# Grouped-query score maps as three fp32r products over 128 rows instead of one plain fp32 product over 64

## The chip, the cores and the metric

The kernel runs on one core of one Trainium2 chip. The metric is the device time of one execution in microseconds (us). TensorE (PE) does the matmuls and the transposes, VectorE (DVE) and ScalarE (ACT) the elementwise work, GpSimd (POOL) small row work and some transfers, and the SyncE (SP) queue the large transfers.

## The reference

Two layers of a hybrid flow-matching backbone on 384 tokens: 256 latent ones (token tiles t=0, 1) and 128 context ones (t=2). Every layer is half a SwiGLU step, a token mixing, and half a SwiGLU step, each between RMS norms that are modulated by a projected condition. What the change touches is the grouped-query part of the mixing:

```python
dq = rms_norm(d_q.reshape(bsz, t, 4, 64), p["gqa_qnorm"][l])   # 4 query heads
dk = rms_norm(d_k.reshape(bsz, t, 2, 64), p["gqa_knorm"][l])   # 2 key heads
# latent tokens: rotary on dq and dk, 128 cached context keys ahead of the own ones
s = jnp.einsum("bqkgd,bskd->bkgqs", qb, k) * 64 ** -0.5
p = jax.nn.softmax(s, axis=-1)
out = jnp.einsum("bkgqs,bskd->bqkgd", p, v)
```

All is float32. Latent queries see 384 keys (128 cached, 256 own), context queries their own 128.

## The kernel before

**Weights.** All weights stream from HBM as 512 KB units on the SP queue (`Stream.load`). ACT casts a unit to fp32r (the high half, L167) and DVE subtracts to get the low half (L168); both write a tile `wu`. A projection is three fp32r matmuls, high by high, high by low and low by high (L556 to L558, L562 to L564, L590 to L592). These fill nearly all of PE's time.

**Order.** A scheduler places each engine's instructions ahead of the run, from the dependences and its own estimates; on an engine they then run in that fixed order, each waiting for semaphores. So the order on an engine is not that of the source.

**The mixing** (`mix`): projections for the convolution branch; then for each token tile the grouped-query projection (into a PSUM tile `ps_j`) and `d_rows`, which squares the rows on ACT (`sqd`), copies the values (`Vg`), sums the squares on DVE (`ss`), gets a reciprocal root on POOL (`rstd`, L470 and L474), scales on DVE (`dn`) and for t<2 applies the rotary on DVE (`dr`, L748 to L757). `d_tail` then transposes the result on PE into a PSUM tile `ps_dT` (L873, L874) and ACT copies it out (L875 queries `qTg` with the scale, L878 keys `kTg`, or `kTgp` for t=2). In `qTg` the two key groups lie on partitions 0 to 63 and 64 to 127. The cached keys come into the first 128 columns of `kTg` by a POOL DMA.

Then twelve units, three token tiles by four heads, software-pipelined over three steps: `probs` makes the score map on PE (`ps_s`, L897), DVE takes the row maximum (L898) and ACT the exponential (`p`, L902); `turned` transposes it (`ps_pT`, L912) and ACT copies (`wt`, L914); `weighted` multiplies with the values (`ps_pv`, L920). Between the units lie the projections of the differential attention (`ps_j`, transposed into `ps_qk`, L1031), and after every unit DVE does four steps of a 31-tap convolution (`cacc`, L825). Twelve units of the differential attention follow, then a norm, and the output projection (`rows_out`).

**Buffers.** `ps_dT`, `ps_pT`, `ps_qk` and some others share two PSUM banks (`mbank`); maps and projections share six (`bank`). Where ACT and DVE both read one PSUM tile, the framework makes the one wait for the other. Sums of squares write their squares to a tile `sink` that nobody reads (L500, L541), and the condition's weights come through two tiles `ast` that DVE multiplies into `acc` (L284, L288).

Of the kernel before, what the change touches and what calls it, by code (L numbers as in the profile page):

```python
# [186 lines left out]
def kernel(ctx: ExitStack, tc: tile.TileContext, a: dict):  # L187
# [7 lines left out]
    ap_ = ctx.enter_context(tc.tile_pool(name="adap", bufs=2))  # L195
# [28 lines left out]
    for t in range(NT):  # L224
# [8 lines left out]
    sink = cp.tile([P, D], BF16, name="sink")  # L233
# [23 lines left out]
    class Ada:  # L257
# [18 lines left out]
        def step(self, pool):  # L276
# [4 lines left out]
            for c in range(2):  # L281
                s1 = sc[:, k, 0, c : c + 1]
# [11 lines left out]
        def finish(self):  # L294
# [13 lines left out]
            else:  # L308
# [12 lines left out]
                grow = tp.tile([P, 512], F32, tag="grow", name=nm("grow"))  # L321
# [76 lines left out]
    def first_mod(q):  # L398
        ps = mbank(nm("ps_first"))
        ws = a0.pop(q)  # L400
        for k in range(KC):
            for s in range(2):
# [3 lines left out]
                    lhsT=sc[:, k, :, :].rearrange("p r i -> p (r i)"),  # L406
# [89 lines left out]
    def pre_norm(t, xn):  # L496
        ss = sm.tile([P, 2], F32, tag="ss", name=nm("ss"))
        for hf in range(2):
            hsl = slice(hf * 512, (hf + 1) * 512)
            nc.scalar.activation(  # L500
                out=sink[:, hsl], in_=x[t][:, hsl], func=AF.Square, scale=D ** -0.5,
                accum_out=ss[:, hf : hf + 1],
            )
# [30 lines left out]
    def post(l, i, t, y):  # L534
# [82 lines left out]
    def ffn(l, i, h, adas, nxt, first=None):  # L617
# [27 lines left out]
        with tc.tile_pool(name=nm("fp"), bufs=1) as fp:  # L645
# [75 lines left out]
    def mix(l, h, nxt):  # L721
        with tc.tile_pool(name=nm("mp"), bufs=1) as mp:
# [13 lines left out]
            nc.gpsimd.dma_start(out=kTg[:, 0:P], in_=a["cache_kT"][l, :, 2])  # L736
# [51 lines left out]
            upad = mp.tile([P, 2, TOK + 3 * CPAD], F32, tag="c3", bufs=4, name=nm("upad"))  # L788
# [22 lines left out]
            cacc = mp.tile([P, 2, TOK + CPAD], F32, tag="c3", bufs=4, name=nm("cacc"))  # L811
# [3 lines left out]
            def conv_some(n):  # L815
                for _ in range(min(n, len(conv_todo))):
# [7 lines left out]
                    else:  # L824
# [3 lines left out]
                        )  # L828

# [104 lines left out]
            def gqa_unit(t, hd, box):  # L934
# [3 lines left out]
                vs = slice(64 * v, 64 * v + 64)  # L938
# [359 lines left out]
```

## Time and profile before

| | |
|---|---|
| median of 3 runs | 1543.93 us (1543.18 to 1545.84) |
| the profiled execution | 1548.72 us, span 1546.9 us |
| granted TensorE clock, mean | 0.993 |
| PE busy | 1492.0 us, 96% |
| DVE busy | 1048.2 us, 68% |
| ACT busy | 635.4 us, 41% |
| POOL busy | 131.4 us, 8% |

The profile is one execution; times in it are us from the start of its span. A group's row gives the line, the engine, the operation, output<-inputs with their shapes, the count, the busy time and the mean of one in ns, then the idle time of the engine just before and what ended it. In a timeline "[1.69 <-DVE dr L757]" behind a row says that the engine sat idle for 1.69 us before it until that instruction released it.

### The profile page before, as it was taken

The page shows a single profiled execution, that of the slowest core. Times are in us where ns is not written, and L with a number is a line of the kernel's source. Part 1 is how long each engine was busy: PE and PEld are TensorE (multiplying, and loading weights), DVE is VectorE, ACT ScalarE, POOL GpSimd, SP SyncE. Part 2 cuts the span into 40 slices and gives each one's busy share as a digit, 9 for nine tenths or more (in the row PEclk, how much of TensorE's full clock was granted, in tenths as well). Part 3 has the DMA queues.
Part 4 walks back from the last instruction along what each step waited for, and adds up shares of the span by engine and source line. Part 5 has one row for each costly group of instructions (what it writes and reads, how often), then busy time and mean ns, then how long its engine had stood idle before and what let it go on. Part 6 is the DMA issues. An engine that isn't in the chain of part 4 may idle for free. (4 is left out here: it accounts for less than half of the span.)

```text
span 1546.9 us, 20700 instructions
## 1 busy us (share of the span) xinstructions
PE 1492.0 (96%) x7924; PEld 1312.3 (85%) x7924; DVE 1048.2 (68%) x1454; ACT 635.4 (41%) x1103; POOL 131.4 (8%) x234
## 2 busy tenths in 40 slices
PE   5999999999999999999999999999999999999997
PEld 3799997777887899998879999887778879999885
DVE  3688889768887846677694666984798785334432
ACT  3442333273575633333263332334545763323331
POOL 1101000021011201000021000001200120000000
PEclk9999999999999999999999999999999999999999
DMA  8678667732224646566655566773322345344431
GB/s 318 231 235 274 228 223 242 242 109 97 69 69 150 204 133 203 201 214 195 197 166 182 183 196 202 234 237 100 124 74 91 108 146 168 123 136 141 134 108 41
DMA packets 73619, 260.13 MB, mean 168 GB/s; under 512 B 9728, under 2 KB 9856, under 8 KB 73520
## 3 DMA queue, kind: packets, MB, share of 16 engines
q1 hardware_dynamic: 68112, 246.32, 48.8%
q0 software_dynamic: 4976, 11.70, 2.8%
q8 instruction: 62, 1.02, 0.3%
q10 hardware_dynamic: 432, 0.79, 0.1%
q14 instruction: 37, 0.30, 0.1%
HBM read 256.36 MB, written 2.41 MB: 167 GB/s over the span
## 5 line engine op out<-in xcount | busy, mean ns | idle before, releaser
L168 DVE TENSOR_TENSOR wu<-st,wu 128x1024 fp32r<-128x1024 f32 x322 | 390.6, 1218 | 258.9 <-ACT wu L167 258.3
L167 ACT CAST wu<-st 128x1024 fp32r<-128x1024 f32 x322 | 337.1, 1052 | 536.2 <-PE ps_f L564 266.4
L562 PE MATMUL ps_f<-h,wu 128*128 128x384 f32 x1248 | 419.0, 336 | 0.0
L564 PE MATMUL ps_f<-h,wu 128*128 128x384 f32 x1248 | 417.1, 334 | 0.0
L563 PE MATMUL ps_f<-h,wu 128*128 128x384 f32 x1248 | 417.1, 334 | 0.0
L288 DVE SCALAR_TENSOR_TENSOR acc<-ast,sc,acc 128x1024 f32<-128x1024 f32 x224 | 279.6, 1281 | 35.0 <-DMA ast<-w_ada 34.6
L562 PEld LDWEIGHTS ps_f<-h,wu 128*128 128x128 f32 x1248 | 234.2, 188 | 7.5 <-issue 7.5
L563 PEld LDWEIGHTS ps_f<-h,wu 128*128 128x128 f32 x1248 | 234.3, 188 | 0.0
L564 PEld LDWEIGHTS ps_f<-h,wu 128*128 128x128 f32 x1248 | 234.2, 188 | 0.0
L590 PE MATMUL ps_o<-wu,hid_s 128*128 128x512 f32 x528 | 207.7, 393 | 0.0
L592 PE MATMUL ps_o<-wu,hid_s 128*128 128x512 f32 x528 | 206.3, 391 | 0.0
L591 PE MATMUL ps_o<-wu,hid_s 128*128 128x512 f32 x528 | 206.2, 391 | 0.0
L590 PEld LDWEIGHTS ps_o<-wu,hid_s 128*128 128x128 f32 x528 | 99.5, 188 | 26.0 <-issue 5.0
L592 PEld LDWEIGHTS ps_o<-wu,hid_s 128*128 128x128 f32 x528 | 99.5, 188 | 21.0
L591 PEld LDWEIGHTS ps_o<-wu,hid_s 128*128 128x128 f32 x528 | 99.6, 189 | 20.3
L702 ACT ACTIVATE sg<-ps_f 128x384 f32<-128x384 f32 x78 | 38.0, 487 | 114.1 <-PE ps_f L564 111.0
L556 PE MATMUL ps_j<-wu,h 128*128 128x512 f32 (+1 forms) x192 | 72.8, 379 | 0.0
L558 PE MATMUL ps_j<-wu,h 128*128 128x512 f32 (+1 forms) x192 | 70.5, 367 | 1.1 <-DVE h L479 1.1
L703 DVE TENSOR_TENSOR hid<-sg,ps_f 128x384 f32<-128x384 f32 x78 | 42.9, 550 | 40.4 <-PE ps_f L564 40.3
L557 PE MATMUL ps_j<-wu,h 128*128 128x512 f32 (+1 forms) x192 | 69.8, 363 | 0.0
L825 DVE SCALAR_TENSOR_TENSOR cacc<-upad,late,cacc 128x399 f32<-128x399 f32 x120 | 69.3, 628 | 0.0
L331 POOL DMA_DIRECT2D gd<-grow x24 | 11.8, 497 | 660.3 <-DVE grow L323 660.3
(234 smaller groups left out, 1698.1 us busy)
## 6 DMA issues: line engine op xcount, KB each, us to landing
st<-ws SPq DMA_DIRECT2D x320, 512.0 KB, 4.3
ast<-w_ada SPq DMA_DIRECT2D x128, 512.0 KB, 4.4
a<-ada SPq DMA_DIRECT2D x16, 512.0 KB, 10.2
G<-gd POOLq DMA_DIRECT2D x12, 512.0 KB, 4.2
brow<-b_ada POOLq DMA_DIRECT2D x24, 64.0 KB, 6.7
prow<-norm_post POOLq DMA_DIRECT2D x24, 64.0 KB, 6.9
x<-x_sample SPq DMA_DIRECT2D x2, 512.0 KB, 5.6
x<-x_prompt SPq DMA_DIRECT2D x1, 512.0 KB, 10.6
```

The lines of the kernel that those rows point to most:

```text
L167: nc.scalar.copy(out=u[:, 0, :], in_=x)
L168: nc.vector.tensor_tensor(out=u[:, 1, :], in0=x, in1=u[:, 0, :].bitcast(F32), op=ALU.subtract)
L288: nc.vector.scalar_tensor_tensor(out=self.acc[c], in0=w, scalar=s1, in1=self.acc[c], op0=ALU.mult, op1=ALU.add)
L556: nc.tensor.matmul(out, lhsT=hk(h, k, 0, tsl), rhs=wh, start=start, stop=False)
L557: nc.tensor.matmul(out, lhsT=hk(h, k, 0, tsl), rhs=wl, start=False, stop=False)
L558: nc.tensor.matmul(out, lhsT=hk(h, k, 1, tsl), rhs=wh, start=False, stop=stop)
L562: nc.tensor.matmul(out, lhsT=wh, rhs=hk(h, k, 0, sl), start=start, stop=False)
L563: nc.tensor.matmul(out, lhsT=wh, rhs=hk(h, k, 1, sl), start=False, stop=False)
L564: nc.tensor.matmul(out, lhsT=wl, rhs=hk(h, k, 0, sl), start=False, stop=stop)
L590: nc.tensor.matmul(out, lhsT=pr[:, 0, s, tsl], rhs=u[:, 0, hsl], start=(q == 0), stop=False)
L591: nc.tensor.matmul(out, lhsT=pr[:, 0, s, tsl], rhs=u[:, 1, hsl], start=False, stop=False)
L592: nc.tensor.matmul(out, lhsT=pr[:, 1, s, tsl], rhs=u[:, 0, hsl], start=False, stop=(q == n - 1))
```

## The change

The score map's queries and keys are kept as fp32r halves (high, low). `qTg` grows to all 128 partitions for each of the four heads: a head's queries lie on its group's 64 partitions and the other 64 hold zeros, which two POOL memsets per layer write at the start of the mixing. `probs` takes lists, and for the grouped-query heads issues three fp32r matmuls, high by high, high by low and low by high, over 128 rows. The differential heads pass lists of one and stay plain fp32.

A helper `halves` makes a pair: ACT writes the high half, DVE subtracts it from the source for the low one. `d_tail` calls it three times per token tile (queries on partitions 0 to 63, queries on 64 to 127, keys) where two ACT copies were; the cached keys come into a tile `kc` and are split once per layer.

To pay for the space, the pool of the `ast` tiles moves from the whole program into `ffn`, `sink` is halved so that both halves of a sum of squares write the same place, `grow` loses its second buffer, and the small tiles `sc` and `upad` are laid out anew.

```diff
-    sink = cp.tile([P, D], BF16, name="sink")
+    sink = cp.tile([P, 512], BF16, name="sink")
...
-        with tc.tile_pool(name=nm("fp"), bufs=1) as fp:
+        with tc.tile_pool(name=nm("fp"), bufs=1) as fp, tc.tile_pool(name=nm("adap"), bufs=2) as ap_:
...
-            kTg = mp.tile([P, TOK], F32, name=nm("kTg"))
-            kTgp = mp.tile([P, P], F32, name=nm("kTgp"))
-            qTg = mp.tile([P, 2, TOK], F32, name=nm("qTg"))
+            kTg = mp.tile([P, 2, TOK], F32R, name=nm("kTg"))
+            kTgp = mp.tile([P, 2, P], F32R, name=nm("kTgp"))
+
+            qTg = mp.tile([P, 2, 4, TOK], F32R, name=nm("qTg"))
+            for v in range(2):
+                z = qTg[64 * (1 - v) : 64 * (1 - v) + 64, :, 2 * v : 2 * v + 2, :]
+                nc.gpsimd.memset(z.bitcast(F32), 0.0)
...
+            def halves(hi, lo, src, scale=1.0):
+                nc.scalar.mul(hi, src, scale)
+                nc.vector.scalar_tensor_tensor(
+                    out=lo, in0=src, scalar=scale, in1=hi.bitcast(F32), op0=ALU.mult, op1=ALU.subtract
+                )
...
+            halves(kTg[:, 0, 0:P], kTg[:, 1, 0:P], kc[:, 0:P])
...
-                nc.scalar.mul(
-                    qTg[:, :, t * P : (t + 1) * P], pt[:, 0:256].rearrange("p (g n) -> p g n", g=2), 64 ** -0.5
-                )
-                nc.scalar.copy(out=kTg[:, (t + 1) * P : (t + 2) * P] if t < 2 else kTgp, in_=pt[:, 256:384])
+                tsl, ksl = slice(t * P, (t + 1) * P), slice((t + 1) * P, (t + 2) * P)
+                for v in range(2):
+                    r, c = slice(64 * v, 64 * v + 64), slice(2 * v, 2 * v + 2)
+                    halves(
+                        qTg[r, 0, c, tsl], qTg[r, 1, c, tsl], pt[r, 0:256].rearrange("p (g n) -> p g n", g=2),
+                        64 ** -0.5,
+                    )
+                k0, k1 = (kTg[:, s, ksl] if t < 2 else kTgp[:, s, :] for s in range(2))
+                halves(k0, k1, pt[:, 256:384])
...
-                nc.tensor.matmul(ps[:, 0:nk], lhsT=lhsT, rhs=rhs, start=True, stop=True)
+                for j, (lt, rt) in enumerate(zip(lhsT, rhs)):
+                    nc.tensor.matmul(ps[:, 0:nk], lhsT=lt, rhs=rt, start=(j == 0), stop=(j == len(rhs) - 1))
...
-                    box[hd] = probs(t, box["st"], hd, qTg[vs, g, tsl], kt[vs, :])
+                    box[hd] = probs(
+                        t, box["st"], hd, [qTg[:, s, hd, tsl] for s in (0, 0, 1)], [kt[:, s, :] for s in (0, 1, 0)]
+                    )
```

The change lets the scheduler order all engines anew. PE, layer 0, where `d_tail` of t=1 and t=2 meets the first maps. Before (ps_dT_3134 is that of t=1, ps_dT_3191 that of t=2, ps_s_3141 and ps_s_3173 the first two maps; L556 to L558 are projections, and the "..." leave out 7 and 10 of them):

```order
L873 MATMUL ps_dT_3134<-early,dr_3048 128x128 x2
L556 MATMUL ps_j_3121<-wu_3111,h_2561 128x512
L557 MATMUL ps_j_3121<-wu_3111,h_2561 128x512
L558 MATMUL ps_j_3121<-wu_3111,h_2561 128x512
L897 MATMUL ps_s_3141<-kTg_2808,qTg_2810 128x384
L556 MATMUL ps_j_3121<-wu_3111,h_2561 128x512
...
L558 MATMUL ps_j_3121<-wu_3116,h_2562 128x512
L897 MATMUL ps_s_3173<-kTg_2808,qTg_2810 128x384
L556 MATMUL ps_j_3178<-wu_2946,h_2559 128x512
...
L558 MATMUL ps_j_3178<-wu_2951,h_2560 128x512
L873 MATMUL ps_dT_3191<-early,dn_3099 128x128 x2
```

The same place in the changed kernel (ps_dT_3146 is t=1, ps_dT_3211 t=2, ps_s_3157 and ps_s_3191 the first two maps; the "..." leaves out 9 projections):

```order
L887 MATMUL ps_dT_3146<-early,dr_3056 128x128 x2
L557 MATMUL ps_j_3133<-wu_3123,h_2563 128x512
...
L558 MATMUL ps_j_3133<-wu_3128,h_2564 128x512
L559 MATMUL ps_j_3133<-wu_3128,h_2564 128x512
L887 MATMUL ps_dT_3211<-early,dn_3111 128x128 x2
L917 MATMUL ps_s_3157<-kTg_2811,qTg_2813 128x384
L917 MATMUL ps_s_3191<-kTg_2811,qTg_2813 128x384
L557 MATMUL ps_j_3198<-wu_2954,h_2561 128x512
L558 MATMUL ps_j_3198<-wu_2954,h_2561 128x512
L917 MATMUL ps_s_3157<-kTg_2811,qTg_2813 128x384 x2
L917 MATMUL ps_s_3191<-kTg_2811,qTg_2813 128x384 x2
```

The transposes of t=2 now stand ahead of the first map, and 12 projections behind those of t=1 instead of 24. DVE at the same place, before (dr_3048 and rt_3049 are the rotary of t=1, ss_3093 and dn_3099 belong to t=2):

```order
L752 TENSOR_TENSOR dr_3048<-dn_3043,late 128x384
L168 TENSOR_TENSOR wu_3116<-st_2944,wu_3116 128x1024
L757 TENSOR_TENSOR dr_3048<-dr_3048,rt_3049 128x384
L840 TENSOR_REDUCE ss_3093<-sqd_3089 128x6
L168 TENSOR_TENSOR wu_3164<-st_2949,wu_3164 128x1024
L846 TENSOR_TENSOR dn_3099<-ps_j_3058,rstd_3097 128x2x2x64
L852 TENSOR_TENSOR dn_3099<-ps_j_3058,rstd_3097 128x128
L857 TENSOR_TENSOR dn_3099<-dn_3099,gqk 128x256
L857 TENSOR_TENSOR dn_3099<-dn_3099,gqk 128x128
L825 SCALAR_TENSOR_TENSOR cacc_2935<-upad_2819,late,cacc_2935 128x399 x2
```

And in the changed kernel (L746 is the low half; ps_dT_3079 is t=0, ps_dT_3146 t=1; "..." leaves out the four dn_3111 rows, which stand as before):

```order
L764 TENSOR_TENSOR dr_3056<-dn_3051,late 128x384
L746 SCALAR_TENSOR_TENSOR qTg_2813<-ps_dT_3079,qTg_2813 64x2x128
L769 TENSOR_TENSOR dr_3056<-dr_3056,rt_3057 128x384
L168 TENSOR_TENSOR wu_3128<-st_2952,wu_3128 128x1024
L746 SCALAR_TENSOR_TENSOR qTg_2813<-ps_dT_3079,qTg_2813 64x2x128
L854 TENSOR_REDUCE ss_3105<-sqd_3101 128x6
L746 SCALAR_TENSOR_TENSOR kTg_2811<-ps_dT_3079,kTg_2811 128x128
L168 TENSOR_TENSOR wu_3182<-st_2957,wu_3182 128x1024
...
L746 SCALAR_TENSOR_TENSOR qTg_2813<-ps_dT_3146,qTg_2813 64x2x128
L837 SCALAR_TENSOR_TENSOR cacc_2941<-upad_2825,late,cacc_2941 128x399
L746 SCALAR_TENSOR_TENSOR qTg_2813<-ps_dT_3146,qTg_2813 64x2x128
L760 TENSOR_TENSOR rt_3177<-ps_j_3133,late 128x32x8 x2
```

The low halves stand between the norm's steps, and the last step of the rotary of t=1 (L769) now stands ahead of a weight unit's low half (L168) instead of behind it. ACT behind the weight cast that follows `Vgp`, with what each row waits for, in the changed kernel (before, the two copies of a token tile stood together and waited for PE only):

```order
L745 ACTIVATE kTg_2811<-ps_dT_3079 128x128 [waits DVE_49]
L745 ACTIVATE qTg_2813<-ps_dT_3146 64x2x128 [waits PE_49]
L745 ACTIVATE qTg_2813<-ps_dT_3146 64x2x128 [waits DVE_49]
L745 ACTIVATE qTg_2813<-ps_dT_3211 64x2x128 [waits PE_49]
L745 ACTIVATE kTg_2811<-ps_dT_3146 128x128 [waits DVE_49]
```

The second high half of a token tile and that of its keys now wait for DVE; the keys of t=1 (the last row), which the first map reads, stand behind the first high half of t=2.

## Rows read from the trace of the kernel before

**Rows 1.** The page: busy time, share of the span and instructions of each engine, and the granted TensorE clock in 40 slices.
```profile
PE 1492.0 (96%) x7924; PEld 1312.3 (85%) x7924; DVE 1048.2 (68%) x1454; ACT 635.4 (41%) x1103; POOL 131.4 (8%) x234
PEclk9999999999999999999999999999999999999999
```

**Rows 2.** PE's waits over the whole run: line, what it waited for, us in total, times, longest.
```profile
PE ps_t L515 <- DVE xn L505: 14.9, 14, 2.7
...
PE ps_dT L873 <- DVE dr L757: 3.4, 2, 1.7
```

**Rows 3.** The score maps, L897, by form (duration in ns min/median/max). The profiler records two passes for each plain fp32 map, so 32 rows are 16 maps of 384 keys and 16 are 8 maps of 128.
```profile
L897 PE MATMUL ps_s<-kTg,qTg x32: 482/535/587, 369.2 to 1151.3; 64*128 64x384 f32 x32
...
L897 PE MATMUL ps_s<-kTgp,qTg x16: 272/322/373, 400.7 to 1166.1; 64*128 64x128 f32 x16
```

**Rows 4.** Timeline of PE at the second map of layer 0: start, duration, instruction.
```profile
371.71 0.39 PE L557 MATMUL ps_j<-wu,h 128*128 128x512 f32 x1
371.94 0.39 PE L558 MATMUL ps_j<-wu,h 128*128 128x512 f32 x1
372.26 0.91 PE L897 MATMUL ps_s<-kTg,qTg 64*128 64x384 f32 x2
373.10 0.50 PE L556 MATMUL ps_j<-wu,h 128*128 128x512 f32 x1
373.43 0.39 PE L557 MATMUL ps_j<-wu,h 128*128 128x512 f32 x1
```

**Rows 5.** Timeline of PE in a SwiGLU stage: fp32r products of 384 columns over 128 rows.
```profile
100.17 0.33 PE L562 MATMUL ps_f<-h,wu 128*128 128x384 f32 x1
100.34 0.33 PE L563 MATMUL ps_f<-h,wu 128*128 128x384 f32 x1
100.51 0.33 PE L564 MATMUL ps_f<-h,wu 128*128 128x384 f32 x1
```

**Rows 6.** Timeline of PE at a map of 128 keys, with the plain fp32 transposes of 128 columns behind it, and fp32r products of 256 columns a little earlier.
```profile
399.46 0.28 PE L557 MATMUL ps_j<-wu,h 128*128 128x256 f32 x1
399.58 0.29 PE L558 MATMUL ps_j<-wu,h 128*128 128x256 f32 x1
...
400.74 0.48 PE L897 MATMUL ps_s<-kTgp,qTg 64*128 64x128 f32 x2
401.16 0.44 PE L929 MATMUL ps_mo<-early,mo 128*128 128x128 f32 x2
401.43 0.60 PE L1031 MATMUL ps_qk<-early,qk 128*128 128x128 f32 x4
401.87 0.78 PE L920 MATMUL ps_pv<-Vg,wt 128*128 128x64 f32 x6
```

**Rows 7.** Timeline of PE where the maps begin, layer 0.
```profile
368.01 0.41 PE L873 MATMUL ps_dT<-early,dr 128*128 128x128 f32 x2 [1.69 <-DVE dr L757]
...
369.15 0.91 PE L897 MATMUL ps_s<-kTg,qTg 64*128 64x384 f32 x2
...
375.97 0.38 PE L873 MATMUL ps_dT<-early,dn 128*128 128x128 f32 x2
...
377.70 0.55 PE L1031 MATMUL ps_qk<-early,qk 128*128 128x128 f32 x3
```

**Rows 8.** Timeline of DVE at the same place.
```profile
366.17 1.22 DVE L168 TENSOR_TENSOR wu<-st,wu 128x1024 fp32r<-128x1024 f32 x1
367.31 0.56 DVE L757 TENSOR_TENSOR dr<-dr,rt 128x384 f32<-128x384 f32 x1
367.77 0.55 DVE L840 TENSOR_REDUCE ss<-sqd 128x6 f32<-128x384 f32 x1
...
370.98 0.42 DVE L846 TENSOR_TENSOR dn<-ps_j,rstd 128x256 f32<-128x256 f32 x1 [1.52 <-POOL rstd L474]
371.52 0.62 DVE L857 TENSOR_TENSOR dn<-dn,gqk 128x256 f32<-128x256 f32 x2
```

**Rows 9.** ACT's copies out of `ps_dT`, by tile (count: duration in ns min/median/max).
```profile
L875 ACT ACTIVATE qTg<-ps_dT x6: 375/378/385, 361.5 to 1132.2; 128x256 f32<-128x256 f32 x6
...
L878 ACT COPY kTg<-ps_dT x4: 256/258/260, 361.8 to 1123.9; 128x128 f32<-128x128 f32 x4
```

**Rows 10.** Groups of DVE, by form: the nearest rows to the low halves (an elementwise step that reads PSUM), and the two reads of one PSUM tile by ACT and DVE.
```profile
L544 DVE TENSOR_TENSOR yg<-ps_o,G 128x512 f32<-128x512 f32 x36 | 24.3, 687 | 23.3 <-ACT sink L541 23.1
...
L846 DVE TENSOR_TENSOR dn<-ps_j,rstd 128x256 f32<-128x256 f32 x6 | 2.5, 425 | 9.1 <-POOL rstd L474 9.1
...
L852 DVE TENSOR_TENSOR dn<-ps_j,rstd 128x128 f32<-128x128 f32 x6 | 1.7, 281 | 0.0
```

**Rows 11.** Busy time of the engines in stretches of layer 0 (length, then PE, PEld, DVE, ACT, POOL busy with instruction counts, the granted clock, the DMA share and GB/s): the grouped-query units are the first three, the differential ones begin with the fourth.
```profile
369.00:385.00 16.00, 15.93 (x73) 10.88 (x73) 14.48 (x30) 6.29 (x17) 2.48 (x3) 1.00 0.27 97
385.00:400.70 15.70, 15.70 (x94) 12.60 (x94) 14.77 (x28) 9.64 (x20) 0.54 (x1) 1.00 0.10 29
400.70:411.30 10.60, 10.60 (x82) 9.88 (x81) 9.52 (x19) 4.46 (x15) 0.00 (x0) 1.00 0.27 95
411.30:430.00 18.70, 18.70 (x96) 15.65 (x96) 14.50 (x32) 9.41 (x27) 0.54 (x1) 0.91 0.29 92
430.00:450.00 20.00, 19.96 (x129) 16.87 (x128) 16.78 (x44) 11.59 (x28) 3.44 (x6) 1.00 0.26 80
```

**Rows 12.** Timeline of POOL at the start of the mixing of layer 0, with its idle time, the memsets of L766 by form, and the time from issue to landing of the cached keys' transfer.
```profile
299.77 0.57 POOL L736 DMA_DIRECT2D kTg<-cache_kT  x1
...
312.48 0.30 POOL L489 TENSOR_SCALAR ms<-ss 128x1 f32<-128x1 f32 x1 [11.88 <-ACT sink L541]
...
L766 POOL MEMSET upad<- x2: 146/146/146, 300.5 to 1055.5; 128x30 f32 x2
L766 POOL MEMSET apad<- x2: 93/93/93, 336.7 to 1091.7; 128x2 f32 x2
...
DMA to landing us min/median/max: 3.2/4.3/5.4
```

**Rows 13.** Timeline of DVE at the end of the mixing of layer 0, and of ACT's two squares at its start.
```profile
491.00 1.28 DVE L288 SCALAR_TENSOR_TENSOR acc<-ast,sc,acc 128x1024 f32<-128x1024 f32 x1 [2.06 <-DMA ast<-w_ada]
...
492.81 1.41 DVE L548 SCALAR_TENSOR_TENSOR x<-yg,rstd,x 128x512 f32<-128x512 f32 x2
...
324.82 0.63 ACT L500 ACTIVATE sink<-x 128x512 bf16<-128x512 f32 x1
...
325.44 0.62 ACT L500 ACTIVATE sink<-x 128x512 bf16<-128x512 f32 x1
```

More of the change, by code (lines that the diff above doesn't have):

```diff
@@ L232 @@
     nc.gpsimd.memset(ones, 1.0)
-    sink = cp.tile([P, D], BF16, name="sink")
+    sink = cp.tile([P, 512], BF16, name="sink")
     scol = setp.tile([P, 16], F32, name="scol")
     nc.scalar.activation(out=scol, in_=early[:, 128:144], func=AF.Silu)
-    sc = cp.tile([P, KC, 16, 2], F32, name="sc")
+    sc = cp.tile([P, KC, 2], F32, name="sc")
+    nc.vector.tensor_copy(out=sc, in_=scol.rearrange("p (i k) -> p k i", i=2))
+    scw = setp.tile([P, KC, 16, 2], F32, name="scw")
     nc.vector.tensor_copy(
-        out=sc,
+        out=scw,
         in_=scol.rearrange("p (i k) -> p k i", i=2).unsqueeze(2).to_broadcast([P, KC, 16, 2]),
@@ L281, in step @@
             for c in range(2):
-                s1 = sc[:, k, 0, c : c + 1]
+                s1 = sc[:, k, c : c + 1]
                 if k == 0:
@@ L320, in finish @@
                     )
-                grow = tp.tile([P, 512], F32, tag="grow", name=nm("grow"))
+                grow = tp.tile([P, 512], F32, tag="grow", name=nm("grow"), bufs=1)
                 nc.vector.tensor_tensor(out=br, in0=br, in1=ps, op=ALU.add)
@@ L500, in pre_norm @@
             nc.scalar.activation(
-                out=sink[:, hsl], in_=x[t][:, hsl], func=AF.Square, scale=D ** -0.5,
+                out=sink, in_=x[t][:, hsl], func=AF.Square, scale=D ** -0.5,
                 accum_out=ss[:, hf : hf + 1],
@@ L541, in post @@
             nc.scalar.activation(
-                out=sink[:, hsl], in_=y[hf], func=AF.Square, scale=D ** -0.5, accum_out=ss[:, hf : hf + 1]
+                out=sink, in_=y[hf], func=AF.Square, scale=D ** -0.5, accum_out=ss[:, hf : hf + 1]
             )
@@ L735, in mix @@
             nc.gpsimd.dma_start(out=kTd[:, :, 0:P], in_=a["cache_kT"][l, :, 0:2])
-            nc.gpsimd.dma_start(out=kTg[:, 0:P], in_=a["cache_kT"][l, :, 2])
+            kc = mp.tile([P, TOK], F32, tag="p", name=nm("kc"), bufs=4)
+            nc.gpsimd.dma_start(out=kc[:, 0:P], in_=a["cache_kT"][l, :, 2])
+            def halves(hi, lo, src, scale=1.0):
[3 more added lines that the diff above has]
+                )
             def rope_apply(dst, src, t, nh, base, hd):
@@ L785, in proj_bank @@
                 return bank(nm("ps_j"))
-            upad = mp.tile([P, 2, TOK + 3 * CPAD], F32, tag="c3", bufs=4, name=nm("upad"))
+            upad = mp.tile([P, 2, TOK + 3 * CPAD], F32, tag="c3u", name=nm("upad"))
             pads(upad, CPAD)
@@ L809, in mix @@
                 later(lambda t=t, u=u: c_tail(t, u), 1)
-            cacc = mp.tile([P, 2, TOK + CPAD], F32, tag="c3", bufs=4, name=nm("cacc"))
+            cacc = mp.tile([P, 2, TOK + CPAD], F32, tag="c3", bufs=3, name=nm("cacc"))
             CW = TOK + CPAD
@@ L937, in gqa_unit @@
                 v, g = hd // 2, hd % 2
-                vs = slice(64 * v, 64 * v + 64)
                 def first():
@@ L1083, in a_fill @@
                     if cc == 0:
-                        ac["p"] = mp.tile([P, 2, TOK + 3], F32, tag="c3", bufs=4, name=nm("apad"))
+                        ac["p"] = mp.tile([P, 2, TOK + 3], F32, tag="c3", bufs=3, name=nm("apad"))
                         pads(ac["p"], 1)
-                        ac["c"] = mp.tile([P, 2, TOK + 1], F32, tag="c3", bufs=4, name=nm("aacc"))
+                        ac["c"] = mp.tile([P, 2, TOK + 1], F32, tag="c3", bufs=3, name=nm("aacc"))
                     apad, aacc = ac["p"], ac["c"]
@@ L1190, in mix @@
             run(flush(True))
-            zT = mp.tile([P, 2, TOK], F32, tag="c3", bufs=4, name=nm("zT"))
+            zT = mp.tile([P, 2, TOK], F32, tag="c3u", name=nm("zT"))
             for t in range(NT):
```

5 lines of the change are left out of this document (2 added, 3 removed).

## The prediction

> **What bounds the kernel now.** I read the page first: PE is busy for 1492.0 of 1546.9 us and its clock is full in all slices [rows 1]. So the time falls by what PE no longer has to do, and rises by each microsecond that PE waits. PE's waits [rows 2] name the two places that matter here: the transposes of normed rows at the stage borders (14.9 us in 14 waits), and the transposes in `d_tail` of t=1, which wait for the rotary on DVE (3.4 us in 2, one per layer). Then I read the stage with the maps as a timeline. In it DVE is nearly as full as PE: over 369.0 to 411.3 us DVE works 14.48 + 14.77 + 9.52 = 38.77 of 42.3 us and is idle for 3.53, while ACT is idle more than half of the time; behind it, over 411.3 to 450, DVE has 18.7 + 20.0 - 14.50 - 16.78 = 7.4 us to spare [rows 11]. The change takes work from PE and gives work to DVE just there.
>
> **The maps of 384 keys.** There are 16 in the run [rows 3]. In the stream, a plain projection product starts every 0.23 us (371.71 to 371.94). Around a map, L558 starts at 371.94, the map at 372.26, L556 at 373.10 and L557 at 373.43, where without the map L557 would start at 371.94 + 2 x 0.23 = 372.40. So a map costs 373.43 - 372.40 = 1.03 us of PE, its passes and the slow starts around them together [rows 4]. Three fp32r products of 384 columns over 128 rows cost 3 x 0.17 = 0.52 us at the spacing of 100.17, 100.34, 100.51 [rows 5]. The new maps have just that form, rows of zeros included. Saving: 0.51 x 16 = 8.2 us.
>
> **The maps of 128 keys.** There are 8. One takes from 400.74 to 401.16, 0.42 us [rows 6], plus a slow start around it, which at the 384 map was about 0.1 us on either side (0.32 and 0.33 against 0.23); so 0.42 to 0.62. No row of before has an fp32r product of 128 columns. The bounds: those of 256 columns start every 0.12 us and fp32 transposes of 128 columns every (401.87 - 401.43) / 4 = 0.11 us [rows 6]; at the other end a pass of the fp32 map itself, 0.42 / 2 = 0.21. Three products: 0.33 to 0.63 us. I take 0.42 against 0.52, a saving of 0.1 x 8 = 0.8 us, near the lower end since the 256-column row is the same kind of product; the ends are a saving of 2.3 and a loss of 1.7.
>
> **What is added on DVE and ACT.** Per token tile, two low halves of 256 elements and one of 128 on DVE. The nearest rows are elementwise steps that read PSUM: 0.42 and 0.28 us [rows 10]. That makes 0.42 + 0.42 + 0.28 = 1.12 us per tile and, with the cached keys' 0.28, 3.65 us per layer. On half the partitions a step could be no longer than that. ACT goes from 0.378 + 0.258 to 0.378 x 2 + 0.258 us [rows 9], which its idle time covers.
>
> The steps also form a chain. The framework makes the second reader of a PSUM tile wait: the 23.1 us that DVE's `yg` waited for ACT's `sink`, on the same `ps_o` and with no data between them, is that [rows 10]. So a token tile's six steps go ACT, DVE, ACT, DVE, ACT, DVE, as the waits in the order show, each with DVE's other queue in between, and `ps_dT`, one of two banks, is held until the last. The Trainium skill, page "PSUM — Partial Sum Buffer", section "PSUM bank collisions raise a hardware error", says that two engines must not access one bank on the same 32 partitions at the same time, reads included, while different partitions of it are free. By that rule the two query halves, on partitions 0 to 63 and 64 to 127, needn't wait for each other, which would take one DVE wait out of the chain. The trace's 23.1 us agree that readers are kept apart; no row shows a pair on different partitions.
>
> **Where the maps begin.** Layer 0, walked by hand from the two timelines [rows 7, 8] and the new order. Before, the transposes of t=1 wait 1.69 us for the rotary, whose last step stands behind a weight unit's low half (1.22 us). Now a low half of 0.42 stands there: the transposes come 0.76 us earlier, near 367.2. But `ss` of t=2 now has a full weight unit and two low halves ahead of it and starts near 368.6 instead of 367.77; the reciprocal root took from 367.77 to 370.98 to be back, so `dn` of t=2 ends near 372.9 (before: 372.05). Before, PE met the transposes of t=2 24 projections later, at 375.97, and didn't wait. Now it meets them after 12, near 367.2 + 0.35 + 12 x 0.23 = 370.3, and waits some 2.5 us. Then the first map wants the high half of the keys of t=1. That stands on ACT behind a high half that waits for a low half on DVE (behind `dn`), and waits for another low half behind a convolution step of 0.6: near 374.4, 1.2 us after the transposes of t=2. At the transposes of `qk` (377.70 before) the changed PE has issued 18 projections and nine map products since the first map: 374.4 + 18 x 0.23 + 9 x 0.17 + 0.4 = 380.5, of which 6 projections (1.4) are work that before came later; and `ps_dT` of t=2, which `qk` needs, comes free near 380.6. So PE is there 380.6 - 1.4 - 377.7 = 1.5 us late, although three maps have already given 1.5 back: the beginning costs about 3.0 us. Before's small waits there (0.5 us, at the first map and at `qk`) are within that. I take 2.5 us a layer, 5.0 for both. The ends: 1.0, if the low halves slip into DVE's idle 1.52 us [rows 8] and the reciprocal root comes sooner; 4.0, if each link of the chain waits for a weight unit.
>
> **The stage behind it.** From 369.0 to 411.3 PE would need 42.3 + 2.5 less eight maps (4.1) and four small ones (0.4), 40.3 us. DVE has 38.77 and gets two of the tiles' halves, 2.24: 41.0. DVE becomes the bound by 0.7 us, seen as late maxima and so late exponentials and transposes. I take 0.8 a layer, 1.6 in all; the ends are nothing (the convolution can slip behind 411.3, where DVE has time) and 4.
>
> **The smaller edits.** The memsets write 1536 elements each; from 2 to 30 elements a memset grows from 93 to 146 ns, 1.9 ns an element [rows 12], so at most 2.9 us each, at least next to nothing. They delay the four transfers behind them on POOL by up to 5.8 us; the last lands by 299.77 + 5.8 + 5.4 = 311 instead of 305, and POOL was idle for 11.88 us before 312.48. With that cover gone the split of the cached keys would hold ACT ahead of a weight cast, some 0.5 us a layer. With `sink` halved, other casts come between a sum's halves (0.63 and 0.62 [rows 13]), and the norm of t=1 and t=2 ends about a cast (1.0 us) later, but the transposes that wait for it stand six matmuls (1.4 us) later too. The `ast` tiles now wait for the mixing's space: the step that waited 2.06 us for one at 491.00 [rows 13] may wait longer, while the `x` update behind it has another order. I take 0 for all of this, with ends of -3 and +3.
>
> **The sum.** -8.2 - 0.8 + 5.0 + 1.6 + 0 = -2.4 us. The profiled execution takes 1548.72 us, so it would take 1546.3; it lies 4.8 above the median of 1543.93, and I take the difference from that: 1541.5 us. About 0.2% (3.1 us) is what a measurement of this kernel can tell from no change, so my forecast is within it, just.
>
> **The rivals.**
> *The chain is hidden (-8.5, 1535.4).* The maps' saving of 9.0 shows nearly whole. For it: DVE's 1.52 us idle at the very place, and the 0.76 us that the rotary gains. Against it: the transposes of t=2 now stand 12 projections earlier, and nothing makes `dn` earlier. Chance 0.2.
> *The stage becomes DVE's (+4, 1548).* At the upper ends of the two terms, 4.0 x 2 + 4 = 12 us against 9.0, or with small maps at 0.63 us (+1.7 instead of -0.8): 12 - 8.2 + 1.7 = 5.5; I take 4. It decides as soon as the beginning and the stage together lose more than 4.5 us per layer, which needs one more weight unit's low half (1.22) in the chain than I walked. For it: DVE's 3.53 us idle against 3.65 added. Chance 0.17.
> *The edits for space decide (+2, 1546).* `ast` arrives late at the end of each mixing and PE's wait for `xn` grows by 2 us or so each, against the gain. Chance 0.08.
> My forecast, 1538.5 to 1545, has 0.55.
>
> **How the numbers follow.** Of the forecast's 0.55, 0.22 lie below 1540.8; with the hidden chain that makes faster 0.42. The rest of it, the third rival's half and a bit of the second give same 0.40, and slower 0.18. The range from 1535 to 1548 holds the forecast, half and more of the first rival and half of the second, and the bounds of the unknown costs put together go no further.
>
> **What would show it.** Right: L917 rows 0.17 us apart and no slow start behind a map; PE's wait at L887 of t=2 near 2.5 us, with releaser `dn`; a wait of the first map for `kTg` L745; DVE over 95% full between the first map and the last. Wrong: no wait at L887 of t=2 (then the first rival), PE waits at L932 for exponentials all through the stage (the second), or longer waits of `xn` and `acc` (the third). If an fp32r product of 128 columns takes over 0.2 us, the small maps cost instead of saving.

## The result, and the profile after

The changed kernel is slower: 1563.52 us median (1561.83 to 1564.85) against 1543.76, a ratio of 1.0109 with an interval of 1.0086 to 1.0133. I had forecast 1541.5 in a range of 1535 to 1548. The profiled execution of after takes 1564.53 us with a span of 1562.8, that of before 1548.72. So what follows accounts for 15.9 us, the difference of the two traces; the medians lie 19.8 apart, since before's profiled execution is 5.0 us above its median.

The page of after: busy time by engine, which barely moved against [rows 1]; PE is busy for 3.3 us more in a span that is 15.9 longer.

```profile
PE 1495.3 (96%) x7948; PEld 1322.2 (85%) x7948; DVE 1055.6 (68%) x1475; ACT 640.4 (41%) x1111; POOL 132.9 (9%) x238
```

To find the place, the n-th product into each kind of PSUM tile is set beside its like in the other trace, since both kernels issue the same projections. How far after lies behind before there, from the starts in the two traces:

| product | before, us | after, us | behind, us | gained or lost since the row above |
|---|---|---|---|---|
| first of SwiGLU 1's output, layer 0 | 226.97 | 226.32 | -0.65 | |
| 60th projection of the mixing | 343.25 | 345.27 | 2.0 | 2.7 lost at the border |
| 157th: behind the transposes of t=1 | 368.28 | 369.47 | 1.2 | 0.8 gained |
| 300th: first differential units | 417.04 | 418.54 | 1.5 | 0.3 lost in the new maps |
| 380th: late in the differential units | 442.62 | 446.65 | 4.0 | 2.5 lost |
| in its output projection | 490.39 | 494.32 | 3.9 | 0.1 gained |
| SwiGLU 2, settled | 527.99 | 534.15 | 6.2 | 2.3 lost at the border |
| SwiGLU 1, layer 1, settled | 826.18 | 834.90 | 8.7 | 2.5 lost at the border |
| mixing, layer 1, settled | 1114.29 | 1125.17 | 10.9 | 2.2 lost at the border |
| behind the transposes of t=1 | 1123.34 | 1133.43 | 10.1 | 0.8 gained |
| differential units begin | 1170.32 | 1182.53 | 12.2 | 2.1 lost in the new maps |
| late in the differential units | 1199.23 | 1214.74 | 15.5 | 3.3 lost |
| end of the mixing | 1244.75 | 1259.50 | 14.8 | 0.7 gained |
| SwiGLU 2, settled, and to the end | 1280.40 | 1296.13 | 15.8 | 1.0 lost at the border |

Within the SwiGLU stages nothing moves. The five borders lose 10.7 us together, the differential units 5.8, and the new maps, which were to save, lose 0.8 net. Of the last two figures 0.84 us per layer is only a shift: a pair of differential maps that costs 0.84 us extra stands ahead of the mark "differential units" in before and behind it in after (shown under "The stage behind it"). Counted alike, the differential units lose 4.1 and the new maps 2.5.

PE's waits in after (line, what it waited for, us in total, times, longest), against [rows 2]: those of the first products for `h` at the borders have grown from 1.7 us (`ps_gu` alone) to 7.6; new are those of the transposes of t=2 for `dn`, of the first map for `kTg`, and of `ps_pv` for an exponential. The wait for the rotary has halved.

```profile
PE ps_t L516 <- DVE xn L506: 14.1, 13, 1.9
...
PE ps_gu L557 <- ACT h L479: 5.4, 4, 1.8
PE ps_dT L887 <- DVE dn L871: 5.1, 2, 2.6
PE ps_s L917 <- ACT kTg L745: 2.3, 2, 1.3
PE ps_j L557 <- ACT h L479: 2.2, 2, 1.1
PE ps_dT L887 <- DVE dr L769: 1.8, 2, 0.9
PE ps_pv L940 <- ACT p L922: 1.7, 2, 0.9
```

The waits are not the whole price. Stretches of after, layer 0 (length; PE, PEld, DVE, ACT, POOL busy; granted clock; DMA share; GB/s): where the maps begin, in the units behind them, and at the border to SwiGLU 2.

```profile
372.30:374.80 2.50, 0.18 (x1) 0.00 (x0) 1.26 (x5) 0.00 (x0) 1.59 (x1) 1.00 0.77 265
374.80:381.60 6.80, 5.62 (x16) 4.69 (x17) 5.90 (x15) 2.99 (x6) 0.62 (x1) 0.50 0.10 39
385.00:415.60 30.60, 30.32 (x222) 27.87 (x220) 30.60 (x59) 17.25 (x42) 0.97 (x2) 1.00 0.18 63
522.00:524.90 2.90, 1.43 (x6) 0.98 (x7) 2.90 (x5) 2.90 (x10) 0.00 (x0) 1.00 0.31 85
524.90:528.40 3.50, 3.50 (x10) 2.75 (x9) 3.49 (x6) 1.25 (x2) 0.60 (x1) 0.52 0.41 131
```

Here the granted clock is 0.50, 1.2 GHz, for 6.8 or 3.4 us behind a stretch in which PE mostly waited. In after there are six such half-clock stretches between the start and the end, 27.3 us, in before two, 6.8 us (at 413.6 and 785.7). PE is busy in most of their time, so I estimate their cost at half their length: 13.7 against 3.4, some 10.2 of the 15.9 us. In the units behind the beginning DVE has no idle time at all (30.60 of 30.60).

Before's stretch at 785.7 stands behind a wait of 2.03 us, but the one at 413.6 stands behind no wait. Two stretches of before around it:

```profile
411.00:413.00 2.00, 2.00 (x8) 1.06 (x8) 2.00 (x5) 1.56 (x5) 0.54 (x1) 1.00 0.32 45
415.00:417.00 2.00, 2.00 (x8) 2.00 (x7) 1.65 (x4) 0.00 (x0) 0.00 (x0) 0.50 0.01 2
```

PE is busy throughout. Just ahead of the fall it does maps over 32 rows and products of 64 columns; kernel 12 below has a half-clock stretch at the same place of layer 1 (1166.8), behind no wait either. No run shows why the clock falls there.

### The profile page after: what moved, and what is told of

Same layout as the page of the kernel before. It is cut to its first block, busy times and chain, and to the rows that moved or that the text cites. A ratio compares the mean times of both kernels' runs of the same rounds, so it can differ in the third digit from the quotient of the medians.

```text
span 1562.8 us, 20833 instructions
## 1 busy us (share of the span) xinstructions
PE 1495.3 (96%) x7948; PEld 1322.2 (85%) x7948; DVE 1055.6 (68%) x1475; ACT 640.4 (41%) x1111; POOL 132.9 (9%) x238
## 5 line engine op out<-in xcount | busy, mean ns | idle before, releaser
L168 DVE TENSOR_TENSOR wu<-st,wu 128x1024 fp32r<-128x1024 f32 x322 | 390.5, 1218 | 262.8 <-ACT wu L167 262.3
L558 PE MATMUL ps_j<-wu,h 128*128 128x512 f32 (+1 forms) x192 | 71.8, 374 | 0.0
```

Of the source, the lines that this page charges most:

```text
L168: nc.vector.tensor_tensor(out=u[:, 1, :], in0=x, in1=u[:, 0, :].bitcast(F32), op=ALU.subtract)
L558: nc.tensor.matmul(out, lhsT=hk(h, k, 0, tsl), rhs=wl, start=False, stop=False)
```

## The experiments

Ratios are to the kernel before, run beside each. Kernels 1 to 4, 5 to 7, 8 to 10 and 11 to 12 each shared a chip.

| kernel | median, us | before, us | ratio and interval |
|---|---|---|---|
| after | 1563.52 | 1543.76 | 1.0109 (1.0086 to 1.0133) |
| 1 before, sink halved | 1557.49 | 1545.26 | 1.0083 (1.0066 to 1.0100) |
| 2 after, old maps | 1556.66 | 1545.26 | 1.0075 (1.0060 to 1.0090) |
| 3 after, full sink | 1552.08 | 1545.26 | 1.0040 (1.0026 to 1.0055) |
| 4 after, 64 rows | 1568.69 | 1545.26 | 1.0151 (1.0136 to 1.0166) |
| 5 as 3, no low halves | 1541.23 | 1546.04 | 0.9960 (0.9946 to 0.9974) |
| 6 as 3, low halves on POOL | 1550.91 | 1546.04 | 1.0026 (1.0016 to 1.0036) |
| 7 as 3, three convolution steps | 1546.66 | 1546.04 | 1.0000 (0.9989 to 1.0010) |
| 8 as 3, keys first | 1543.93 | 1545.94 | 0.9989 (0.9977 to 1.0001) |
| 9 as 8, three convolution steps | 1543.07 | 1545.94 | 0.9982 (0.9970 to 0.9995) |
| 10 as 3, zeros in the keys | 1549.31 | 1545.94 | 1.0020 (1.0009 to 1.0030) |
| 11 as 9, `d_tail` due earlier | 1544.13 | 1545.59 | 0.9991 (0.9981 to 1.0002) |
| 12 before, three convolution steps | 1548.31 | 1545.59 | 1.0016 (1.0006 to 1.0025) |

### 1 to 3: the borders

Kernel 1 is before with this edit alone:

```diff
-    sink = cp.tile([P, D], BF16, name="sink")
+    sink = cp.tile([P, 512], BF16, name="sink")
...
-                out=sink[:, hsl], in_=x[t][:, hsl], func=AF.Square, scale=D ** -0.5,
+                out=sink, in_=x[t][:, hsl], func=AF.Square, scale=D ** -0.5,
...
```

> The kernel before with one edit of the change alone: sink halved, so that both halves of a sum of squares write one place. Borders theory: this edit makes the scheduler put the transposes of the second and third token tile later at the borders between stages, PE runs out of work there and its clock falls to half; the trace of after lost 2.7, 2.3, 2.4, 2.2 and 1.1 us at the five borders, so 1554 us (+10), with waits of 1.1 to 1.8 us of the first product for h, and two to four half-clock stretches of 3.4 us more than before. Maps theory (all loss comes from the new maps and what they do to DVE): 1544 us, no difference.

Kernel 2 is after with `kTg`, `qTg`, `d_tail` and `probs` as before:

> The changed kernel with the old plain fp32 maps: all edits for space (sink halved, the ast tiles' pool in ffn, one grow, small tiles), no halves, no zeros. Borders theory with sink as the cause: the same as with sink halved alone, 1554 us, within 1.5 us. If the move of the ast tiles costs too, more than that: 1556 to 1558. Maps theory: 1544.

Kernel 3 is after with the edit of kernel 1 taken back:

> The changed kernel with sink at its full size again, all else as changed. Borders theory: the borders are as before, the grouped-query and differential stages keep what the trace of after lost there (2.0 us in layer 0, 3.9 in layer 1): 1550 us, half-clock stretches of 6.8 us left where the maps begin, none at the borders beyond those of before. Maps theory: 1563, as changed.

Kernel 1 is slower by 0.83%, 12.8 us, kernel 2 no more than that, and kernel 3 is 0.69%, 10.7 us, below after (the two intervals leave some 4 us of play). Halving `sink` alone accounts for the borders; the move of the `ast` tiles costs nothing that shows beside it. The timeline of ACT in kernel 1 at the border to SwiGLU 2 shows what happens: a weight cast stands between the two squares of one sum (first view), where in before they were neighbours at the same border (second view), as they were at the start of the mixing [rows 13].

```profile
502.50 0.64 ACT L500 ACTIVATE sink<-x 128x512 bf16<-128x512 f32 x1
503.04 0.20 ACT L500 ACTIVATION_READ_ACCUMULATOR sink<-x 128x1 f32 x1
503.13 1.04 ACT L167 CAST wu<-st 128x1024 fp32r<-128x1024 f32 x1
504.07 0.63 ACT L500 ACTIVATE sink<-x 128x512 bf16<-128x512 f32 x1
```

```profile
501.75 0.64 ACT L500 ACTIVATE sink<-x 128x512 bf16<-128x512 f32 x1
...
502.38 0.63 ACT L500 ACTIVATE sink<-x 128x512 bf16<-128x512 f32 x1
```

The order of PE in kernel 1 has 34 products between the transposes of the second and the third token tile there, where before had 23. So the third tile's `h` comes late, and PE runs out of other work; its timeline:

```profile
516.97 1.09 PE L515 MATMUL ps_t<-early,xn 128*128 128x128 f32 x8 [0.68 <-DVE xn L505]
517.81 0.47 PE L556 MATMUL ps_gu<-wu,h 128*128 128x512 f32 x1
518.13 0.39 PE L557 MATMUL ps_gu<-wu,h 128*128 128x512 f32 x1
518.36 0.40 PE L558 MATMUL ps_gu<-wu,h 128*128 128x512 f32 x1
520.29 0.50 PE L556 MATMUL ps_gu<-wu,h 128*128 128x512 f32 x1 [1.54 <-ACT h L478]
```

Three products cover the transposes' way through ACT, which takes longer. That the scheduler splits the squares because the second now overwrites the first's output is argued from the edit, not shown. The four executions of kernel 1 went from 1553.38 us at a mean clock of 0.996 to 1559.63 at 0.989. Only the first was traced; it has one half-clock stretch (335.7) and is still 8.1 us above before's median, so most of these 8.1 are waits. That the others differ by the clock behind the same waits is likely from their means, but not shown.

### 4: is it the zeros?

Kernel 4 packs the queries as before and drops the zeros; its new lines against after:

```diff
...
+            qTg = mp.tile([P, 2, 2, TOK], F32R, name=nm("qTg"))
...
+                halves(
+                    qTg[:, 0, :, tsl], qTg[:, 1, :, tsl], pt[:, 0:256].rearrange("p (g n) -> p g n", g=2),
+                    64 ** -0.5,
+                )
...
+                        t, box["st"], hd, [qTg[vs, s, g, tsl] for s in (0, 0, 1)], [kt[vs, s, :] for s in (0, 1, 0)]
...
```

> The changed kernel with maps of three fp32r products over 64 rows: the queries packed as before, so no zeros, no memsets, and two pairs of halves per token tile (0.42 + 0.28 us on DVE) instead of three. Chain theory: one wait for DVE and 0.42 us of DVE less per tile; the transposes of t=2 wait 0.3 to 0.8 us less and PE gains 2 to 4 us in all, 1560 us, as long as PE's clock still falls where the maps begin; if it no longer falls there, up to 8 us, 1555. If fp32r over 64 rows costs PE more than over 128 (rows 0.17 us apart in after), slower: an fp32 pass took 0.42 us, and at that price 24 x 2 x 0.25 = 12 us more, 1575.

Slower than after, 1.0151 against 1.0109: the direction of the third case, at half its size. PE at 64 rows in kernel 4, then three products over 128 rows in after, both at full clock:

```profile
392.54 0.44 PE L912 MATMUL ps_s<-kTg,qTg 64*128 64x384 f32 x1
392.91 0.55 PE L927 MATMUL ps_pT<-early,p 128*128 128x128 f32 x3
393.38 0.61 PE L912 MATMUL ps_s<-kTg,qTg 64*128 64x384 f32 x2
393.93 0.50 PE L557 MATMUL ps_j<-wu,h 128*128 128x512 f32 x1
```

```profile
382.95 0.69 PE L917 MATMUL ps_s<-kTg,qTg 128*128 128x384 f32 x3
383.48 0.40 PE L557 MATMUL ps_j<-wu,h 128*128 128x512 f32 x1
```

Over 64 rows one product takes 0.37 us and two take 0.55; over 128 rows three take 0.53 (0.61 where they stand behind `ps_pv`) and the next product starts at once. So the slow start around a map [rows 4] is there for fp32r over 64 rows too and gone with the zeros. Here no transpose waits for `dn`, but the first map waits longer for the keys (3.34 us in both layers against 0.96 and 1.32), so the time of kernel 4 mixes the two.

### 5 to 7: the low halves, and DVE

Kernel 5 leaves out DVE's subtraction in `halves` and multiplies the high halves three times.

> The changed kernel with sink at full size, and the low halves left out: DVE does nothing in d_tail, nothing waits between ACT and DVE there, and each map multiplies the high halves three times (so the maps lack their low parts). PE has the same number of products as changed. Chain theory (the loss left with a full sink, 1552 against 1545, comes from the low halves on DVE: the late dn, the waits of the first map, the clock that falls there, and late exponentials in the differential units): PE's saving shows whole, 8 to 9 us below before, 1536 to 1537, no wait of 2.5 us at the transposes of t=2, no half-clock stretch there. Rival (the loss comes from the other edits, the ast tiles, kc or the memsets): 1550 to 1552, with the same waits.

Faster than before by 0.40%, 6.2 us (the medians lie 4.8 apart), and 0.80% below kernel 3: the low halves, with the order that they bring, cost more than the maps save. In kernel 5 the transposes of t=2 stand behind the first two maps again, as in before, so it doesn't part DVE's work from that order; kernel 8 does. No wait for `dn` is left and, in the profiled execution, no half-clock stretch where the maps begin. It did not reach 8 to 9 us: `qk` waits 1.1 us per layer for the copies out of `ps_dT`, and two pairs of differential maps per layer are broken where before breaks one (0.84 us each, below).

Kernel 6 gives the subtraction to POOL:

```diff
-            def halves(hi, lo, src, scale=1.0):
+            def halves(hi, lo, src, full, scale=1.0):
...
-                nc.vector.scalar_tensor_tensor(
-                    out=lo, in0=src, scalar=scale, in1=hi.bitcast(F32), op0=ALU.mult, op1=ALU.subtract
-                )
+                nc.gpsimd.tensor_tensor(out=lo, in0=full, in1=hi.bitcast(F32), op=ALU.subtract)
...
```

> The changed kernel with sink at full size; ACT copies queries and keys out of ps_dT to SBUF in fp32 (as before), makes the high halves from that copy, and POOL subtracts for the low ones, so DVE has no part in it and ps_dT is free after ACT's two copies. Chain theory: as without low halves, less what POOL adds: PE's saving of 8 to 9 us, less 1 to 3 us of waits for POOL, 1538 to 1541, faster than before. If POOL takes over 1.5 us for a subtraction of 256 elements (a memset of 1536 took 1.38), the first map waits 3 us and more in each layer and the clock falls again: 1546 to 1552.

The time came out as in the second case, though a subtraction of 256 elements takes about 0.8 us, the longest 1.18. Timeline of POOL and then of DVE in kernel 6:

```profile
363.05 1.62 POOL L746 TENSOR_TENSOR qTg<-qf,qTg 64x256 fp32r<-64x256 f32 x2
364.75 1.53 POOL L746 TENSOR_TENSOR kTg<-qf,kTg 128x128 fp32r<-128x128 f32 x1
374.11 0.46 POOL L746 TENSOR_TENSOR kTg<-qf,kTg 128x128 fp32r<-128x128 f32 x1
```

```profile
363.66 1.16 DVE L869 TENSOR_TENSOR dn<-dn,gqk 128x256 f32<-128x256 f32 x2
364.75 1.21 DVE L168 TENSOR_TENSOR wu<-st,wu 128x1024 fp32r<-128x1024 f32 x1
```

While both work, one of them is slow: DVE's two steps take 1.16 us instead of 0.62 [rows 8], and POOL's 128 elements 1.53 beside a weight unit of the usual 1.21. At 374.11 POOL's step takes 0.46 (with DVE idle, at 305.17, 0.45), and the convolution step that began with it 0.89 instead of 0.62. So the rotary came late again (PE waited 2.5 us for it, 1.7 in before) and the first map 1.9 and 2.9 us for POOL; in layer 0 the clock fell behind both waits (368.8 and 375.6).

Kernel 7 changes `CONV1` from 4 to 3 in kernel 3.

> The changed kernel with sink at full size and three convolution steps behind each unit instead of four, so that about a quarter of the convolution leaves the grouped-query units for the differential ones, where DVE has 7 us idle. If DVE's load in the stage is what is left to pay behind the first maps (2.5 and 3.3 us in the differential units of the two layers): 1547, 5 us below the full sink alone; the waits where the maps begin stay (2.5 and 1.3 us). If only those waits and the clock behind them cost: 1552, no difference.

0.40% below kernel 3, as expected if DVE's load costs; the waits at the beginning stayed (2.55 and 0.97 to 1.32 us), the waits for exponentials in the differential units went. Kernel 12 is before with that edit alone:

> The kernel before with three convolution steps per unit instead of four, nothing else. In before DVE was full but not late in the grouped-query units (3.53 us idle of 42.3, no wait of PE for a maximum), so if the 5 us that three steps gave the changed kernel come from DVE being its bound there, before gains little: 1544 to 1547, no difference. If three steps are simply the better order for the differential units, before gains as much: 1540 to 1542.

Before gets no faster by it, 0.16% slower. So three steps are not a better order as such; they relieve a DVE that the low halves had filled.

### 8 to 11: the chain where the maps begin

Kernel 8 is kernel 3 with the keys' halves ahead of the queries':

```diff
+                k0, k1 = (kTg[:, s, ksl] if t < 2 else kTgp[:, s, :] for s in range(2))
+                halves(k0, k1, pt[:, 256:384])
                 for v in range(2):
...
-                k0, k1 = (kTg[:, s, ksl] if t < 2 else kTgp[:, s, :] for s in range(2))
-                halves(k0, k1, pt[:, 256:384])
```

> The changed kernel with sink at full size and one edit: d_tail makes the halves of the keys ahead of those of the queries, with the same six steps. The first map needs the keys of t=1, so its chain loses two pairs of steps. In the order the transposes of t=2 stand 24 products behind those of t=1 again, as before, instead of 12. If the beginning of the maps (waits of 2.5 and 1.3 us per layer and half-clock stretches of 3.4 to 6.8 us behind them) is what the full sink alone still pays: the waits go, the clock stays full there, and 1552 falls by 6 to 9 us to 1543 to 1546. If the load on DVE is what costs, whatever stands first: 1550 to 1552, with the waits moved elsewhere.

From 1.0040 to 0.9989, 7.9 us, by an order of six steps. The work on DVE is the same; what changed is that the first map's chain is short, and that the scheduler puts the transposes of t=2 behind the first maps again and breaks no pair of differential maps (kernel 3 breaks one per layer, 1.7 us in both). PE's waits in kernel 8:

```profile
PE ps_s L917 <- DVE kTg L746: 2.8, 2, 1.4
PE ps_pv L940 <- ACT wt L934: 2.5, 2, 1.3
PE ps_s L917 <- ACT kTg L745: 2.4, 2, 1.2
PE ps_dT L887 <- DVE dr L769: 1.6, 2, 0.8
```

These are 9.3 us, where kernel 3 waits 11.1 at the same places (5.1 for `dn`, 2.5 for the keys, 1.8 for the rotary, 1.7 at `ps_pv`), but none is over 1.5 us, and in its profiled execution the clock stayed full from the start to the end. Kernel 3's has 13.7 us at half clock, by the estimate above 6.8 of the 9.2 us between the two traces. Kernel 8's other executions have mean clocks of 0.992 to 0.998, so the clock falls in some of them too.

Kernel 9 is kernel 8 with `CONV1` at 3:

> Keys first and three convolution steps per unit together, with the full sink. If the two causes are separate (the chain where the maps begin, DVE's load behind it), their gains add: 5 us from the convolution and 6 to 9 from the keys, 1538 to 1541, faster than before by 4 to 7 us. If they are one (a late DVE), the sum is little better than the better of the two: 1543 to 1546.

Kernel 9 is 0.9982 of before, 2.8 us faster and clear of its interval: a version that beats both. The gains did not add, as expected if the two edits relieve the same late DVE. That isn't parted from the pairs: kernel 9 breaks one per layer again, kernel 8 none.

Kernel 10 puts the zeros in the keys:

> The full sink, and the zeros in the keys' other half instead of the queries': keys in two copies per group with zeros, made first (two pairs of halves of 128 elements on 64 partitions), queries packed (one pair of 256 elements on 128 partitions). DVE's work per token tile falls from 1.12 to 0.98 us and the order has the transposes of t=2 24 products later and the pairs of differential maps together. Chain theory: as with keys first or a little better, 1541 to 1545. If the memsets (now also of the keys) or the cached keys' halves hold something: 1546 to 1550.

The last case, 1.0020: the first map still waits 0.9 and 2.3 us per layer (kernel 8: 1.2 and 1.4), and there the clock fell again; the transposes of `p` wait 3.6 us for exponentials in both layers together. I have no run that says why it waits longer with less work on DVE.

Kernel 11 is kernel 9 with `D_LAG` at 2:

> The full sink, keys first, three convolution steps per unit, and d_tail due two steps after its projection instead of three. In the order the three products of a map stand together (with keys first alone, the first map's first product stands 8 projections ahead of its other two) and no wait for the keys' high half should be left. If the waits that keys first leaves (1.2 and 1.4 us per layer) come from the order of d_tail: 1538 to 1540, 3 to 5 us below keys first with three steps. If the rotary of t=1 is simply late on DVE: the waits move to the transposes of d_tail, 1542 to 1545.

No better than kernel 9 within the intervals: the waits moved to the transposes of t=0 and t=1 (1.5 and 1.0 us), the last case.

## Why the prediction was wrong, point by point

**The maps on PE were right.** Three products of 384 columns take 0.53 us in the stream of projections (382.95 to 383.48 above), against 0.52 forecast, and 0.61 behind `ps_pv`. Those of 128 columns start 0.13 to 0.14 us apart, what the forecast took (0.42 for three):

```profile
404.22 0.31 PE L917 MATMUL ps_s<-kTgp,qTg 128*128 128x128 f32 x1
404.36 0.51 PE L932 MATMUL ps_pT<-early,p 128*128 128x128 f32 x3
404.63 0.42 PE L917 MATMUL ps_s<-kTgp,qTg 128*128 128x128 f32 x2
404.89 0.41 PE L949 MATMUL ps_mo<-early,mo 128*128 128x128 f32 x2
```

**The waits where the maps begin were right, their price was not.** Forecast: the transposes of t=1 0.76 us sooner, 2.5 us of wait for `dn`, 1.2 for the keys. Measured, layer 0:

```profile
369.20 0.41 PE L887 MATMUL ps_dT<-early,dr 128*128 128x128 f32 x2 [0.88 <-DVE dr L769]
375.02 0.66 PE L887 MATMUL ps_dT<-early,dn 128*128 128x128 f32 x2 [2.54 <-DVE dn L871]
376.86 0.98 PE L917 MATMUL ps_s<-kTg,qTg 128*128 128x384 f32 x2 [0.96 <-ACT kTg L745]
```

The step that failed is "I take 2.5 us a layer, 5.0 for both", which prices a wait at its length. Behind these waits came 6.8 us at half clock in each layer, some 3.4 us more per layer. Before's trace had shown such stretches, 3.4 us at 785.7 behind a wait of 2.03 and the window of 0.91 in [rows 11]; I read past both. The reading "its clock is full in all slices" was wrong: a digit 9 stands for 0.90 and more, and 3.4 us at half clock leave a slice of 38.7 us at 0.96. Without the half-clock stretches of both traces, as an estimate, the two layers would stand at -2.2 and -2.1 us from the start of the mixing to the differential units, and at -1.4 and -1.3 with the shifted pair counted alike, where the forecast had -1.2 each. So the rest of that sum came out; that each term did is not shown.

**"I take 0 for all of this, with ends of -3 and +3"** is the term that failed most. I had seen casts between the squares and weighed a cast's 1.0 us against six matmuls at the second tile's transposes. I didn't follow the third tile, whose transposes moved 11 products later (34 against 23) with the work behind them used up. It measured 10.7 us (kernel 3 against after).

**The stage behind it.** DVE did become the bound (30.60 of 30.60 us busy). But a loss fell in the differential units, 2.5 and 3.3 us by the table, where I had put none (my 0.8 per layer was for the stage ahead of them): that the convolution can slip to "where DVE has time" was no cover, for exponentials came late there. Part of the two figures is the shift named above. PE in kernel 3, whose order there is that of after, at the second pair of differential maps of layer 1, then the first two pairs in before:

```profile
1174.47 0.91 PE L917 MATMUL ps_s<-kTd,qTd 32*128 32x384 f32 x2
1175.31 0.33 PE L932 MATMUL ps_pT<-early,p 128*128 128x128 f32 x1
1175.57 0.91 PE L917 MATMUL ps_s<-kTd,qTd 32*128 32x384 f32 x2
1176.41 0.44 PE L563 MATMUL ps_j<-h,wu 128*128 128x384 f32 x1
```

```profile
1166.32 0.91 PE L897 MATMUL ps_s<-kTd,qTd 32*128 32x384 f32 x2
1167.16 0.43 PE L920 MATMUL ps_pv<-Vgp,wt 128*128 128x64 f32 x2
1167.52 0.91 PE L897 MATMUL ps_s<-kTd,qTd 32*128 32x384 f32 x2
...
1173.34 0.92 PE L897 MATMUL ps_s<-kTd,qTd 32*128 32x384 f32 x4
1174.18 0.44 PE L562 MATMUL ps_j<-h,wu 128*128 128x384 f32 x1
```

Two maps side by side take 0.84 us, as long as one alone, so an instruction between them costs 0.84. Before, after and kernel 3 each break one of eight pairs per layer: before the first, ahead of the mark in the table, the others the second, behind it. So the broken pair is no loss of the change. Of the 3.3 us of layer 1, 0.84 are this shift and 1.4 the waits of 0.85 and 0.58 us for exponentials; where the other 1.0 went is open.

**The rivals.** The second, "the stage becomes DVE's", had the direction and the place but forecast 1548; with the full sink it measured 1552. The third, the edits for space, had the border but named `ast`, which cost nothing that shows; it was `sink`. The chance of 0.18 for slower came from pricing each mishap alone, though all of them feed one engine's waits and several waits brought a slower clock.

**The PSUM rule.** By the rule that the forecast names from the Trainium skill, "PSUM — Partial Sum Buffer", section "PSUM bank collisions raise a hardware error", the query halves needn't wait for each other. No run here tried it, since the framework writes that wait. Kernel 8 shows that the place in the chain matters; no run changes the chain's length alone.

## What to carry to other kernels

An edit for space that lets two steps write the same scratch is an edit of the order: look at what the scheduler does with all that stands behind it, to the last tile. Where PE is full, price a wait by its length and by what the clock does behind it, and look for half-clock stretches in windows of a few us, not in the page's digits. And in a chain between engines, put first what the next stage reads first: six steps in another order gave 7.9 us here, clock and pairs included, about what the maps were to save.

## What the runs showed of the hardware

- The clock has two levels and falls behind many waits, not behind all: of single waits of 1.5 to 2.7 us some were followed by 3.4 or 6.8 us at 0.50 (2.54 in after at 372.5), others by none (2.67 in before at 494.4). In kernel 3 a fall at 428.5 stands behind a wait of 0.85, in before the one at 413.6 behind none. The Trainium skill, "TensorE: Matmul & The Clock Gate", section "What's actually happening", says that the array's clock is passed at half or full rate by how busy the engine has been; the trace agrees on the two levels (0.50 and 1.00, 27.3 us of half clock in after), but the fall at 413.6, with PE busy throughout in the profile, does not follow from it.
- fp32r products over 64 rows cost more among products over 128 than those over 128 with zeros: 0.37 us for one and 0.55 for two, against 0.53 to 0.61 for three.
- Maps over different 32-row groups run at the same time when nothing stands between them (four passes in 0.84 us, as two), and one after the other with one product or transpose between them (0.84 each). The Trainium skill, "TensorE: Matmul & The Clock Gate", section "Part 3: Packing small matmuls — row/col tiling", says of small row tiles that they run at once in the array; the trace agrees.
- Of DVE and POOL, both on SBUF operands, one is slowed while the other works: two DVE steps from 0.62 to 1.16 us, a POOL step from 0.46 to 1.53. The Trainium skill, "SBUF — State Buffer", section "SBUF: two separate sides", has them sharing a port pair that one holds for a whole instruction; the trace agrees: the POOL step of 1.53 us began with the weight unit of 1.21 and ended 0.32 us behind it.
